# First stage of a diffusion layer kernel: squares in tiles of their own, eight tiles summed by TensorE instead of four, and a new order of its 528 steps

## The chip, the cores and the metric

The kernel runs on one core of a Trainium2 chip. What is measured is the device time of one execution in microseconds (us), as the median over several runs. A core has five engines, each with an instruction queue of its own that is worked in order: TensorE (PE in the profile; its weight loads are listed apart as PEld), VectorE (DVE), ScalarE (ACT), GpSimd (POOL) and SyncE (SP). In this kernel SP issues the loads, and 16 DMA engines carry them out.

## The reference

One layer of a diffusion transformer: 512 latent tokens and 256 context tokens of width 2048. Both are normalised and modulated, projected, attended in two ways, and go through a gated MLP. The change lies in the first lines alone:

```python
def _rmsnorm(x, w):
    xf = x.astype(jnp.float32)
    y = xf * lax.rsqrt(jnp.mean(xf * xf, axis=-1, keepdims=True) + EPS)
    return y.astype(x.dtype) * w
...
mod_x = (sc_ @ w_ada[l] + b_ada[l])[:, None, :]
mod_c = (scc @ w_ada[l] + b_ada[l])[None, None, :]
...
h = _modulate(_rmsnorm(x, norm1_w[l]), sh1, s1)
hc = _modulate(_rmsnorm(xc, norm1_w[l]), sh1c, s1c)
...
p = h @ w_in
```

So each token needs the sum of its 2048 squares, and each of the 2048 features needs a scale and a shift, which are dot products of the conditioning vectors with rows of `w_ada`.

## The kernel before, in words

The tokens stand in the free direction, the features in the 128 partitions: 16 feature tiles `kt`, each 512 latent columns (x) and 256 context columns (c) wide. Two neighbouring tiles make a pair; pair p holds tiles 2p and 2p+1. The first stage does the following.

- **Loads** (SP, lines 423 to 539): x in 16 loads of 256 KB into `a4k` tiles, the context in 8 loads into `c4k` tiles, then for each feature tile one row block of `w_ada` of 1 MB (`ada`, three buffers), for each pair four blocks `adak` of 512 KB (four buffers), and for each feature tile a weight block `wr` of 320 KB (two buffers).
- **Sum of squares.** For each pair ScalarE squares x (line 454) and, for pairs 0 to 3, the context (line 460); VectorE squares the context of pairs 4 to 7 (line 458). Pair 0 goes to the tile `ccb`, the others to two buffers `h` in turn. VectorE adds pairs 1 to 6 to `ccb`, one instruction of 1536 columns for each (line 465). TensorE then multiplies `ccb` and the last pair by a matrix of ones and adds up over partitions in a PSUM tile `s` (line 472: two column halves of 512 and 256 for each of two tiles of two pairs, 8 matmuls in all).
- **Wide rows.** TensorE spreads the two conditioning vectors over all partitions (line 487), and ScalarE copies them into the tiles `cb` and `ccb` (line 491). For the context vector the target is `ccb`, so this copy comes after TensorE has read the sum of squares there.
- **Root** (lines 502 to 511): ScalarE computes the reciprocal root by Ln and Exp (502, 504) and two factors (505, 507); VectorE sharpens it by one Newton step into `rinv` (509, 511), the 512 latent columns first, then the 256 context columns.
- **Scales and shifts.** Scale: TensorE multiplies the `adak` blocks (554), ScalarE copies (558), TensorE picks the columns (562), ScalarE finishes them (568). Shift of 14 of the 16 tiles: VectorE takes two dot products of 2048 columns with an `ada` block (619; one with `cb`, one with `ccb`). Shift of tiles 1 and 8 ("turned"): TensorE transposes the `ada` block in four groups (582), ScalarE copies each (585), TensorE multiplies (591), ScalarE copies (594), TensorE picks (599), ScalarE finishes (604).
- **Normalised tiles.** VectorE multiplies by `rinv` (640), ScalarE modulates (646) and rounds to the high part (652), VectorE takes the low part (654). The weights are split likewise (541 on ScalarE, 542 on VectorE).
- **Features.** For each of the 16 feature tiles TensorE does five groups of three matmuls with 512 latent columns and four groups of three with 256 context columns (`mm3`, lines 286 to 288). They add up in PSUM over the whole stage.

Every step is recorded in a list with a number, and `FIRST_ORDER` (line 74) is a table of these numbers: the steps are issued in its order, which fixes the order on every engine. After the first stage the kernel goes on with code that is the same in both versions.

Of the kernel before, what the change touches and what calls it, by code (L numbers as in the profile page):

```python
# [9 lines left out]
F32 = mybir.dt.float32  # L10
# [54 lines left out]
class Step:  # L65
# [6 lines left out]


FIRST_ORDER = (
# [24 lines left out]


ATTENTION_ORDER = (
# [83 lines left out]
class Flow:  # L185
# [7 lines left out]
    def buf(self, make, ring=None, count=None):  # L193
        if ring:
            self.rings[ring] = count
        return Buf(ring, make)
# [26 lines left out]
def layer_kernel(ctx: ExitStack, tc: tile.TileContext, small, rope, c_row, cc_row, x_t, ctx_t, ada, ada_k,  # L223
# [170 lines left out]
    def none():  # L394
        return buf(lambda: None)
# [14 lines left out]
    def xv(kts):  # L410
        return sel_(xr[kts[0] // 2], kts)

    def cv(kts):
        k = kts[0] % 2
        return cr[kts[0] // 4]()[:, kts[0] // 2 % 2, k:k + len(kts)]
# [17 lines left out]
    step("ACT", 1.3, 3.0, lambda: sc.preload_act_table_set("natural_log_exp_and_others"))  # L433
    step("ACT", 0.2, 3.1, lambda: sc.activation(ls, ls, AF.Exp))
    ssq = buf(s_tile, "s", 2)
    LAST = (7,)
    ON_DVE = (4, 5, 6, 7)

    def h_buf():
        return buf(lambda: st.tile([P, 2 * TT], F32, tag="h", name=nm("h"), bufs=2), "h", 2)  # L440

    def hv(t, kts, i):
        n_ = len(kts)
        if i:
            return t[:, 2 * T:2 * T + n_ * C].rearrange("p (k c) -> p k c", k=n_)
        return t[:, :n_ * T].rearrange("p (k t) -> p k t", k=n_)

    taken = buf(lambda: ccb)
    qs = [taken] + [h_buf() for _ in range(7)]
    for p in range(8):  # L450
        t, q, kts = 3.5 + 2 * p, qs[p], (2 * p, 2 * p + 1)
        flow.part = f"q{p}"
        for k in range(2):
            step("ACT", 0.63, t + 0.7 * k, lambda q=q, kts=kts, k=k: sc.square(hv(q(), kts, 0)[:, k], xv(kts)[:, k]),
                 r=[at_x[kts[k]]], w=[q], hold=[xr[p]])
        def ctx_square(q=q, kts=kts, p=p):
            if p in ON_DVE:
                ve.tensor_tensor(hv(q(), kts, 1), cv(kts), cv(kts), op=ALU.mult)
            else:
                sc.square(hv(q(), kts, 1), cv(kts))  # L460

        step(*(("DVE", 0.7) if p in ON_DVE else ("ACT", 0.64)), t + 0.6, ctx_square, r=[at_c[kts[0]], at_c[kts[1]]],
             w=[q], hold=[cr[p // 2]])
        if p and p not in LAST:
            step("DVE", 1.77, t + 1.8, lambda q=q: ve.tensor_tensor(
                ccb[:, :2 * TT], ccb[:, :2 * TT], q(), op=ALU.add), r=[q], w=[taken])
    flow.part = "q"
    sums = [0, *LAST]
    for i, p in enumerate(sums):
        for k in range(2):  # L470
            for m, (c0, c1, cost) in enumerate(((0, T, 1.0), (T, TT, 0.5))):
                step("PE", cost, 20.0 + i + 0.1 * k, lambda m=m, p=p, c0=c0, c1=c1, i=i, k=k: pe.matmul(
                    ssq()[:, c0:c1], ones32, hv(qs[p](), (0, 1), m)[:, k], start=i == 0 and k == 0,
                    stop=i == len(sums) - 1 and k == 1), r=[qs[p]], w=[ssq])
    wide = [[none() for _ in range(4)] for _ in range(2)]
    for i, t in enumerate((cb, ccb)):
        flow.part = f"b{i}"
        s_ = buf(s_tile, "s", 2)
        for j in range(4):
            d = s_ if j < 2 else buf(b_tile, "b", 4)  # L480

            def view(d=d, j=j):
                return d()[:, j * 512:j * 512 + 512] if j < 2 else d()

            def rows_of(i=i, j=j, view=view):
                for k in range(4):
                    pe.matmul(view()[:, k * P:(k + 1) * P], cpad[:, 4 * j + k, i:i + 1].to_broadcast([P, P]), ident,
                              start=True, stop=True)

            step("PE", 1.0, 5.0 + 18 * i + j, rows_of, r=[pad], w=[d])  # L490
            step("ACT", 0.57, 8.0 + 18 * i + j, lambda t=t, o=slice(j * 512, j * 512 + 512), view=view: sc.copy(
                t[:, o], view()), r=[d], w=[wide[i][j]] + [taken] * i)

    flow.part = "r"
    rinv = st.tile([P, TT], F32, name="rinv")
# [2 lines left out]
    for k, (c0, c1) in enumerate(((0, T), (T, TT))):  # L498
        r, s, g = rinv[:, c0:c1], slice(c0, c1), 1 - 0.38 * k
        br = none()  # L500
        t = 24.0 + 0.1 * k
        step("ACT", 0.7 * g, t, lambda r=r, s=s: sc.activation(r, ssq()[:, s], AF.Ln, bias=epst, scale=1.0 / D),
             r=[ssq], w=[br])
        step("ACT", 0.63 * g, t, lambda r=r: sc.activation(r, r, AF.Exp, scale=-0.5), w=[br])
        step("ACT", 0.65 * g, t, lambda s=s: sc.activation(nt[0]()[:, s], ssq()[:, s], AF.Identity, bias=epst, scale=1.0 / D),
             r=[ssq], w=[nt[0]])
        step("ACT", 0.65 * g, t, lambda r=r, s=s: sc.activation(nt[1]()[:, s], r, AF.Square, scale=math.sqrt(0.5)),
             r=[br, ssq], w=[nt[1]])
        step("DVE", 0.69 * g, t, lambda s=s: ve.tensor_tensor(nt[1]()[:, s], nt[1]()[:, s], nt[0]()[:, s], op=ALU.mult),
             r=[nt[0]], w=[nt[1]])  # L510
        step("DVE", 0.69 * g, t, lambda r=r, s=s: ve.scalar_tensor_tensor(
            out=r, in0=nt[1]()[:, s], scalar=1.5, in1=r, op0=ALU.subtract, op1=ALU.mult), r=[nt[1]], w=[br])
        at_r.append(br)
# [188 lines left out]
    step("X", 0.0, T0 + 200, lambda: None, needs=[s for s in flow.steps if s.eng == "PE"], hold=[*xh, *xl, *ch])  # L702
    with tc.manual_schedule(engines={mybir.EngineType.PE, mybir.EngineType.Activation, mybir.EngineType.DVE,
                                     mybir.EngineType.SP, mybir.EngineType.Pool}):
        for i in FIRST_ORDER:
            flow.steps[i].fn()
    ve.tensor_tensor(neglam, ls[:, 1:2], ls[:, 0:1], op=ALU.subtract)
# [1554 lines left out]
```

## Time and profile before

| | us |
|---|---|
| median of 3 runs (2326.39 to 2332.14) | 2327.16 |
| the profiled execution | 2327.31 |
| its span, from first to last instruction | 2325.5 |
| TensorE busy | 2288.4 (98%) |
| VectorE busy | 1725.2 (74%) |
| ScalarE busy | 1164.3 (50%) |

A row of a timeline gives the start in us from the span's start, the duration, the engine, the line, the operation and its operands (output<-inputs), then how many neighbouring instructions are merged, and in brackets the idle time ahead of it with what ended that. A row of the windows gives, for a stretch of time, its length, then the busy time of PE, PEld, DVE, ACT and POOL with the number of instructions, the share of full speed that the clock of TensorE was granted, the share of time in which the DMA engines were busy, and GB/s.

### The profile page before, as it was taken

To read this page: it belongs to the slowest core of one execution; us is meant where nothing else is said; L and a number is where in the kernel's file an instruction comes from. 1 tells how busy PE (TensorE), PEld (TensorE's weight loads), DVE (VectorE), ACT (ScalarE), POOL (GpSimd) and SP (SyncE) were. 2 spreads that over 40 slices of the span, in tenths; PEclk is the share of its full clock that TensorE was granted. 3 is DMA by queue.
4 is the path that set the end of the run, shared out by engine and by line. 5 is a ranking of instruction groups with operands and counts; after the bars stand their busy time and mean duration, and the time that the engine had idled before them with its cause. 6 is when DMAs were issued, how large, how long until landed. Compare 5 with 4: busy or idle time off the path is not lost.

```text
span 2325.5 us, 32178 instructions
## 1 busy us (share of the span) xinstructions
PE 2288.4 (98%) x12378; PEld 1959.2 (84%) x12378; DVE 1725.2 (74%) x2206; ACT 1164.3 (50%) x1777; POOL 265.6 (11%) x308
## 2 busy tenths in 40 slices
PE   6999999999999999999999999999999999999998
PEld 5788888888888888898888888888888888888887
DVE  7988775699877677796676758585858585867667
ACT  6542211577776522454554545454545454545455
POOL 0000001200133121000101010101010101010110
PEclk8999999999999999999999999999999999999999
DMA  9978888646201299335646463746464646554663
GB/s 360 366 259 303 317 296 292 183 132 210 81 25 37 96 348 359 104 117 136 148 126 143 130 161 101 175 114 160 121 154 127 142 131 145 141 144 123 159 184 102
DMA packets 124731, 404.23 MB, mean 174 GB/s; under 512 B 14337, under 2 KB 18945, under 8 KB 114081
## 3 DMA queue, kind: packets, MB, share of 16 engines
q1 hardware_dynamic: 96658, 346.92, 44.9%
q0 software_dynamic: 26768, 54.21, 12.6%
q8 instruction: 97, 1.59, 0.3%
q10 hardware_dynamic: 1152, 1.05, 0.1%
q14 instruction: 56, 0.46, 0.1%
HBM read 332.45 MB, written 69.67 MB: 173 GB/s over the span
## 4 chain that ended last, share of the span: by engine, by line
PE 94%; DVE 3%; ACT 1%; DMA 1%; issue 1%; SPq 0%; DVEq 0%; ACTq 0%
PE y L1959 12%; PE b L286 11%; PE b L287 11%; PE b L288 11%; PE y L1961 6%; PE z L1959 6%; PE s L1025 4%; PE s L286 3%; PE s L287 3%; PE s L288 3%; PE z L1961 3%; PE x L1959 3%; PE pt L1045 2%; PE f L286 2%; PE f L287 2%; PE f L288 2%
## 5 line engine op out<-in xcount | busy, mean ns | idle before, releaser
L1719 DVE TENSOR_TENSOR wl<-wr,wh 128x1024 fp32r<-128x1024 f32 x144 | 177.0, 1230 | 137.1 <-ACT wh L1711 136.4
L1984 POOL DMA_DIRECT2D x_d<-xs x160 | 139.6, 994 | 1148.4 <-ACT xs L1983 1146.4
L286 PE MATMUL b<-ah,wh 128*128 128x512 f32 (+1 forms) x664 | 256.8, 387 | 0.0
L287 PE MATMUL b<-al,wh 128*128 128x512 f32 (+1 forms) x664 | 256.7, 387 | 0.0
L1711 ACT CAST wh<-wr 128x1024 fp32r<-128x1024 f32 x144 | 150.7, 1048 | 211.3 <-PE b L287 100.9
L288 PE MATMUL b<-ah,wl 128*128 128x512 f32 (+1 forms) x664 | 255.8, 385 | 0.0
L1719 DVE TENSOR_TENSOR wl<-rb,wh 128x1024 fp32r<-128x1024 f32 x123 | 150.0, 1219 | 120.6 <-ACT wh L1711 120.6
L1719 DVE TENSOR_TENSOR wl<-ws,wh 128x1024 fp32r<-128x1024 f32 x123 | 150.4, 1222 | 110.6 <-ACT wh L1711 110.6
L1711 ACT CAST wh<-rb 128x1024 fp32r<-128x1024 f32 x123 | 129.2, 1051 | 174.1 <-PE b L287 80.0
L1959 PE MATMUL y<-a2k,wh 128*128 128x512 f32 x656 | 164.1, 392 | 0.4 <-DVE m L1658 0.4
L1711 ACT CAST wh<-ws 128x1024 fp32r<-128x1024 f32 x123 | 128.4, 1044 | 71.1 <-PE b L287 48.5
L288 PEld LDWEIGHTS b<-ah,wl 128*128 128x128 f32 x664 | 124.8, 188 | 25.7
L286 PEld LDWEIGHTS b<-ah,wh 128*128 128x128 f32 x664 | 125.1, 188 | 22.9
L287 PEld LDWEIGHTS b<-al,wh 128*128 128x128 f32 x664 | 125.1, 188 | 22.0
L1959 PEld LDWEIGHTS y<-a2k,wh 128*128 128x128 f32 x656 | 118.6, 189 | 22.2 <-issue 0.5
L250 ACT CAST wh<-wr 128x1024 fp32r<-128x1024 f32 x51 | 53.5, 1052 | 162.3 <-DMA wr<-in_w_o 47.8
L1959 PE MATMUL y<-b2k,wh 128*128 128x512 f32 x410 | 106.8, 390 | 0.0
L1983 ACT ACTIVATE xs<-b,modx 128x512 f32<-128x512 f32 x160 | 101.7, 681 | 5.4 <-DMA x_d<-xs 5.4
L1030 ACT ACTIVATE p<-s,m 128x768 f32<-128x768 f32 x96 | 86.6, 903 | 30.7 <-DVE m L1028 28.6
L1028 DVE TENSOR_REDUCE m<-s 128x1 f32<-128x768 f32 x96 | 90.6, 950 | 6.8 <-PE s L1025 6.4
L1961 PEld LDWEIGHTS y<-a2k,wl 128*128 128x128 f32 x656 | 89.5, 190 | 6.4
L1961 PE MATMUL y<-a2k,wl 128*128 128x256 f32 x656 | 91.5, 282 | 0.0
(530 smaller groups left out, 5929.9 us busy)
## 6 DMA issues: line engine op xcount, KB each, us to landing
ada<-in_ada SPq DMA_DIRECT2D x80, 1024.0 KB, 7.3
rb<-in_w_up SPq DMA_DIRECT2D x123, 512.0 KB, 4.4
wr<-in_w_dn SPq DMA_DIRECT2D x88, 512.0 KB, 3.6
x_d<-xs POOLq DMA_DIRECT2D x160, 256.0 KB, 6.0
wr<-in_w_up SPq DMA_DIRECT2D x53, 512.0 KB, 4.3
wr<-in_w_f SPq DMA_DIRECT2D x34, 512.0 KB, 6.3
adak<-in_ada_k SPq DMA_DIRECT2D x32, 512.0 KB, 7.8
wr<-in_w_o SPq DMA_DIRECT2D x32, 512.0 KB, 5.3
```

What stands on the lines that cost most here:

```text
L286: pe.matmul(out, st[0], mv[0], start=start, stop=False, **kw)
L287: pe.matmul(out, st[0], mv[1], start=False, stop=False, **kw)
L288: pe.matmul(out, st[1], mv[0], start=False, stop=stop, **kw)
L1025: pe.matmul(s()[:, c0:c1], a, b[:, c0:c1], start=i == 0, stop=i == len(ms) - 1)
L1028: step("DVE", 0.87, t + cost + 0.2, lambda: ve.tensor_reduce(out=m(), in_=s()[:, :TT], axis=AX.X, op=ALU.max, negate=True), r=[s], w=[m])
L1030: step("ACT", 0.9, t + cost + 1.2, lambda: sc.activation(p(), s()[:, :TT], AF.Exp, bias=m(), accum_out=lcol()), r=[s, m], w=[p, l], lag=0.25)
L1711: sc.copy(t, raw[:, k * n_:k * n_ + n_])
L1719: ve.tensor_tensor(t, raw[:, k * n_:k * n_ + n_], hi[k].bitcast(F32), op=ALU.subtract)
L1959: pe.matmul(o, w[j][0], hs[j], start=start and j == 0, stop=False, skip_group_check=True)
L1961: pe.matmul(o[:, h0], w[j][1], hs[j][:, h0], start=False, stop=j == 7, skip_group_check=True)
L1983: sc.mul(x, po, modx[:, 80 + dt:81 + dt])
L1984: gp.dma_start(x1_d[dt], x, accum_op=ALU.add)
```

## The change

The squares no longer go to `ccb` and `h`. Eight tiles `sx` (from the `a4k` buffers) and four tiles `sq_c` (from the `c4k` buffers) hold all of them, made ahead of everything else. VectorE does four additions of pairs instead of six: pair 0 to 1, 1 to 2, 2 to 3 and 4 to 5, each in two instructions (1024 columns of x, 512 of the context). TensorE multiplies four pairs by ones instead of two: 3, 5, 6 and 7, so 16 matmuls instead of 8. The x and context halves are waited for apart. The copies into `ccb` no longer wait for anything of the squares. Line numbers of the changed kernel are one to twelve higher: 423 is now 424, 472 is 482, 582 is 592, 619 is 629, 286 is 287.

```diff
-    LAST = (7,)
     ON_DVE = (4, 5, 6, 7)
+    ADDS = ((0, 1), (1, 2), (2, 3), (4, 5))
...
-    taken = buf(lambda: ccb)
-    qs = [taken] + [h_buf() for _ in range(7)]
+    sx, sq_c = [a4k(F32) for _ in range(8)], [c4k(F32) for _ in range(4)]
...
-        if p and p not in LAST:
-            step("DVE", 1.77, t + 1.8, lambda q=q: ve.tensor_tensor(
-                ccb[:, :2 * TT], ccb[:, :2 * TT], q(), op=ALU.add), r=[q], w=[taken])
...
+    for a, b in ADDS:
+        for i, cost in enumerate((1.22, 0.69)):
+            flow.part = f"q{b}"
+            step("DVE", cost, 5.3 + 2 * b, lambda a=a, b=b, i=i: ve.tensor_tensor(
+                square_of(b, i), square_of(b, i), square_of(a, i), op=ALU.add), r=[squares[i][a]], w=[squares[i][b]],
+                 hold=[homes[i][a], homes[i][b]])
+    sums = [none() for _ in range(2)]
+    roots = [p for p in range(8) if p not in [a for a, _ in ADDS]]
+    for p in roots:
         for k in range(2):
...
+                    ssq()[:, c0:c1], ones32, square_of(p, i)[:, k], start=p == roots[0] and k == 0,
+                    stop=p == roots[-1] and k == 1), r=[squares[i][p]], w=[sums[i]], hold=[ssq, homes[i][p]])
...
-                t[:, o], view()), r=[d], w=[wide[i][j]] + [taken] * i)
+                t[:, o], view()), r=[d], w=[wide[i][j]])
...
+        for b in (*sx, *sq_c):
+            b()
         for i in FIRST_ORDER:
             flow.steps[i].fn()
```

The table itself is new from end to end; its first line was

```diff
-    2, 0, 3, 6, 5, 1, 24, 4, 8, 11, 27, 65, 9, 30, 73, 7, 31, 10, 28, 29, 12, 71, 32, 14, 69, 34, 13, 33, 35, 20,
+    0, 22, 4, 6, 2, 24, 3, 5, 26, 89, 7, 50, 9, 27, 13, 32, 16, 83, 28, 8, 30, 75, 11, 31, 10, 51, 87, 1, 35,
```

On SP, these rows stood at the end of the x loads before (`wr`, `ada` and `adak` are the weight blocks of above):

```order
L425 DMA c4k_250<-in_ctx_t 128x512 x2
L423 DMA a4k_257<-in_x_t 128x512 x2
L539 DMA wr_268<-in_w_g 128x640
L539 DMA wr_273<-in_w_g 128x640
L527 DMA ada_276<-in_ada 128x2048
L527 DMA ada_285<-in_ada 128x2048
L532 DMA adak_295<-in_ada_k 128x1024
```

Now they are:

```order
L426 DMA c4k_188<-in_ctx_t 128x512
L549 DMA wr_237<-in_w_g 128x640
L424 DMA a4k_244<-in_x_t 128x512
...
L537 DMA ada_269<-in_ada 128x2048
L424 DMA a4k_282<-in_x_t 128x512
L424 DMA a4k_286<-in_x_t 128x512
...
L537 DMA ada_301<-in_ada 128x2048
L549 DMA wr_314<-in_w_g 128x640
L542 DMA adak_318<-in_ada_k 128x1024
L542 DMA adak_323<-in_ada_k 128x1024
L549 DMA wr_330<-in_w_g 128x640
```

One weight block and one `ada` block have moved ahead of the last four x loads. After `wr_330` come two more `adak` blocks and then `ada_343`, the block of the turned tile 1.

On VectorE, the end of the squares and the Newton step of the root before (`junk` marks a dot product, `modx` its result for latent, `modc` for context tokens; each is followed by a short instruction that is left out here):

```order
L465 TENSOR_TENSOR ccb<-ccb,h_279 128x1536
L542 TENSOR_TENSOR wl_300<-wr_268,wh_289 128x640
L542 TENSOR_TENSOR wl_307<-wr_273,wh_291 128x640
L458 TENSOR_TENSOR h_293<-c4k_250 128x512
...
L619 ISA junk_313,modx<-ada_276,cb,smt 128x2048
...
L619 ISA junk_326,modx<-ada_285,cb,smt 128x2048
...
L619 ISA junk_345,modc<-ada_276,ccb,smt 128x2048
...
L619 ISA junk_365,modc<-ada_285,ccb,smt 128x2048
...
L509 TENSOR_TENSOR h_362<-h_362,h_355 128x512
L511 SCALAR_TENSOR_TENSOR rinv<-h_362,rinv 128x512
```

and now:

```order
L464 TENSOR_TENSOR c4k_183<-c4k_186 128x512
L473 TENSOR_TENSOR a4k_177<-a4k_177,a4k_176 128x1024
L629 ISA junk_311,modx<-ada_269,cb,smt 128x2048
...
L629 ISA junk_325,modc<-ada_269,ccb,smt 128x2048
...
L629 ISA junk_335,modc<-ada_301,ccb,smt 128x2048
...
L629 ISA junk_345,modx<-ada_301,cb,smt 128x2048
...
L552 TENSOR_TENSOR wl_357<-wr_314,wh_341 128x640
L519 TENSOR_TENSOR h_359<-h_359,h_348 128x512
L521 SCALAR_TENSOR_TENSOR rinv<-h_359,rinv 128x512
L552 TENSOR_TENSOR wl_385<-wr_330,wh_362 128x640
L519 TENSOR_TENSOR h_359<-h_359,h_348 128x256
```

The Newton step still stands behind four dot products, but the second of them now takes the context vector, and one weight split stands ahead of the Newton step.

On TensorE, from the last sum of squares to the first features before (`b_335<-ident,ada` are the transposes of the turned tile, `c4k` and `a4k` the normalised tiles):

```order
L472 MATMUL s_297<-h_293,ones_85 128x256
L554 MATMUL b_335<-adak_295,cpad 32x256 x4
L554 MATMUL b_335<-adak_310,cpad 32x256 x4
L554 MATMUL b_335<-adak_304,cpad 32x256 x4
L554 MATMUL b_335<-adak_317,cpad 32x256 x4
L562 MATMUL b_335<-sel,row 128x2 x2
L582 MATMUL b_335<-ident,ada_330 128x128 x8
L591 MATMUL b_335<-wt_382,cpad 32x128 x8
L582 MATMUL b_335<-ident,ada_330 128x128 x4
L286 MATMUL s_432<-a4k_414,wh_289 128x512
```

and now:

```order
L482 MATMUL s_288<-a4k_179,ones_85 128x512 x2
L482 MATMUL s_288<-c4k_182,ones_85 128x256
L482 MATMUL s_288<-c4k_183,ones_85 128x256 x4
L564 MATMUL b_364<-adak_323,cpad 32x256 x4
...
L572 MATMUL b_364<-sel,row 128x2 x2
L592 MATMUL b_364<-ident,ada_343 128x128 x8
L287 MATMUL b_423<-c4k_410,wh_362 128x256
L288 MATMUL b_423<-c4k_410,wh_362 128x256
L289 MATMUL b_423<-c4k_410,wl_385 128x256
...
L601 MATMUL b_364<-wt_412,cpad 32x128 x8
```

Features of the context now stand between the groups of the turned tile, ahead of those of the latent tokens. From the first transpose of the turned tile 1 to the first products with `adak` blocks of the third pair, TensorE has the same instructions in both versions, in another order. In the rest of the stage the products with `adak` blocks stand further back among the features: those of the fourth pair at row 146 of TensorE's order instead of row 128, those of the fifth at 193 instead of 172, those of the seventh at 327 instead of 303.

More of the change, by code (lines that the diff above doesn't have):

```diff
@@ L446, in hv, with square_of @@
         return t[:, :n_ * T].rearrange("p (k t) -> p k t", k=n_)
-    taken = buf(lambda: ccb)
-    qs = [taken] + [h_buf() for _ in range(7)]
+    def square_of(p, i):
+        return sq_c[p // 2]()[:, p % 2] if i else sx[p]()
+    sx, sq_c = [a4k(F32) for _ in range(8)], [c4k(F32) for _ in range(4)]
+    squares = [[none() for _ in range(8)] for _ in range(2)]
+    homes = [sx, [sq_c[p // 2] for p in range(8)]]
     for p in range(8):
-        t, q, kts = 3.5 + 2 * p, qs[p], (2 * p, 2 * p + 1)
+        t, kts = 3.5 + 2 * p, (2 * p, 2 * p + 1)
@@ L452, in layer_kernel, with ctx_square @@
         flow.part = f"q{p}"
         for k in range(2):
-            step("ACT", 0.63, t + 0.7 * k, lambda q=q, kts=kts, k=k: sc.square(hv(q(), kts, 0)[:, k], xv(kts)[:, k]),
-                 r=[at_x[kts[k]]], w=[q], hold=[xr[p]])
-        def ctx_square(q=q, kts=kts, p=p):
+            step("ACT", 0.59, t + 0.7 * k, lambda p=p, kts=kts, k=k: sc.square(square_of(p, 0)[:, k], xv(kts)[:, k]),
+                 r=[at_x[kts[k]]], w=[squares[0][p]], hold=[xr[p], sx[p]])
+        def ctx_square(kts=kts, p=p):
@@ L457, in ctx_square @@
             if p in ON_DVE:
-                ve.tensor_tensor(hv(q(), kts, 1), cv(kts), cv(kts), op=ALU.mult)
+                ve.tensor_tensor(square_of(p, 1), cv(kts), cv(kts), op=ALU.mult)
             else:
-                sc.square(hv(q(), kts, 1), cv(kts))
-        step(*(("DVE", 0.7) if p in ON_DVE else ("ACT", 0.64)), t + 0.6, ctx_square, r=[at_c[kts[0]], at_c[kts[1]]],
-             w=[q], hold=[cr[p // 2]])
-        if p and p not in LAST:
-            step("DVE", 1.77, t + 1.8, lambda q=q: ve.tensor_tensor(
-                ccb[:, :2 * TT], ccb[:, :2 * TT], q(), op=ALU.add), r=[q], w=[taken])
@@ L467, in layer_kernel @@
-    flow.part = "q"
-    sums = [0, *LAST]
-    for i, p in enumerate(sums):
+                sc.square(square_of(p, 1), cv(kts))
+        step(*(("DVE", 0.7) if p in ON_DVE else ("ACT", 0.6)), t + 0.6, ctx_square, r=[at_c[kts[0]], at_c[kts[1]]],
+             w=[squares[1][p]], hold=[cr[p // 2], sq_c[p // 2]])
+    for a, b in ADDS:
[4 more added lines that the diff above has]
+                 hold=[homes[i][a], homes[i][b]])
@@ L470, in layer_kernel @@
+    sums = [none() for _ in range(2)]
+    roots = [p for p in range(8) if p not in [a for a, _ in ADDS]]
+    for p in roots:
+        flow.part = f"p{p}"
         for k in range(2):
[L471 to L474, printed above, removed]
+            for i, (c0, c1, cost) in enumerate(((0, T, 1.2), (T, TT, 0.62))):
+                step("PE", cost, 6.0 + 2 * p + 0.1 * k, lambda i=i, p=p, c0=c0, c1=c1, k=k: pe.matmul(
+                    ssq()[:, c0:c1], ones32, square_of(p, i)[:, k], start=p == roots[0] and k == 0,
+                    stop=p == roots[-1] and k == 1), r=[squares[i][p]], w=[sums[i]], hold=[ssq, homes[i][p]])
@@ L502, in layer_kernel @@
         step("ACT", 0.7 * g, t, lambda r=r, s=s: sc.activation(r, ssq()[:, s], AF.Ln, bias=epst, scale=1.0 / D),
-             r=[ssq], w=[br])
+             r=[sums[k]], w=[br], hold=[ssq])
         step("ACT", 0.63 * g, t, lambda r=r: sc.activation(r, r, AF.Exp, scale=-0.5), w=[br])
         step("ACT", 0.65 * g, t, lambda s=s: sc.activation(nt[0]()[:, s], ssq()[:, s], AF.Identity, bias=epst, scale=1.0 / D),
-             r=[ssq], w=[nt[0]])
+             r=[sums[k]], w=[nt[0]], hold=[ssq])
         step("ACT", 0.65 * g, t, lambda r=r, s=s: sc.activation(nt[1]()[:, s], r, AF.Square, scale=math.sqrt(0.5)),
-             r=[br, ssq], w=[nt[1]])
+             r=[br], w=[nt[1]])
         step("DVE", 0.69 * g, t, lambda s=s: ve.tensor_tensor(nt[1]()[:, s], nt[1]()[:, s], nt[0]()[:, s], op=ALU.mult),
```

47 rows, old and new, of the table FIRST_ORDER are left out of this document.

## The prediction

> **What bounds the kernel now.** I read the page first, then the busy time by stretches, then the timelines of the first 60 us. The page:
>
> ```profile
> span 2325.5 us, 32178 instructions
> ...
> PE 2288.4 (98%) x12378; PEld 1959.2 (84%) x12378; DVE 1725.2 (74%) x2206; ACT 1164.3 (50%) x1777; POOL 265.6 (11%) x308
> ```
>
> TensorE idles 2325.5 - 2288.4 = 37.1 us in all. The stretches say where (the fourth column is PE's busy time, then PEld, DVE, ACT, POOL, the granted clock, the DMA share and GB/s):
>
> ```profile
> 10.00:20.00 10.00, 5.14 (x37) 4.76 (x35) 8.96 (x7) 8.47 (x17) 0.00 (x0) 0.92 1.05 405
> 20.00:30.00 10.00, 6.35 (x14) 3.55 (x15) 9.82 (x11) 4.59 (x8) 0.00 (x0) 0.57 1.02 424
> 30.00:40.00 10.00, 7.01 (x73) 4.39 (x71) 8.05 (x11) 7.99 (x17) 0.00 (x0) 0.95 1.01 391
> 40.00:50.00 10.00, 8.28 (x59) 6.53 (x52) 9.23 (x13) 4.78 (x11) 0.00 (x0) 0.71 1.00 380
> 53.00:147.00 94.00, 93.45 (x679) 74.95 (x678) 86.99 (x89) 51.05 (x88) 1.46 (x2) 1.00 0.86 318
> 147.00:300.00 153.00, 153.00 (x718) 127.83 (x717) 124.60 (x172) 45.02 (x67) 0.00 (x0) 1.00 0.81 293
> ```
>
> From 53 us on TensorE is full. What the change can win lies ahead of that: idle time of TensorE, and work done at a clock of 0.57 or 0.71. After the stage, TensorE has the same instructions in the same order in both kernels and no idle time in the 153 us that follow, so I let whatever the first stage gains pass through to the end unchanged. The early path on TensorE (start, duration, idle time ahead in brackets):
>
> ```profile
> 23.65 5.31 PE L472 MATMUL s<-ccb,ones 128*128 128x512 f32 x8 [6.54 <-DVE ccb L465]
> ...
> 30.54 1.89 PE L472 MATMUL s<-h,ones 128*128 128x256 f32 x6
> 32.36 1.93 PE L554 MATMUL b<-adak,cpad 128*32 128x256 f32 x32
> 35.23 0.61 PE L562 MATMUL b<-sel,row 128*128 128x2 f32 x4 [0.93 <-ACT row L558]
> 36.54 0.66 PE L582 MATMUL b<-ident,ada 128*128 128x128 f32 x4 [0.70 <-ACT a L568]
> 37.87 0.66 PE L582 MATMUL b<-ident,ada 128*128 128x128 f32 x4 [0.68 <-ACT wt L585]
> 39.20 1.08 PE L591 MATMUL b<-wt,cpad 128*32 128x128 f32 x16 [0.68 <-ACT wt L585]
> 42.00 1.11 PE L582 MATMUL b<-ident,ada 128*128 128x128 f32 x4 [1.72 <-ACT row L594]
> ...
> 58.44 1.07 PE L554 MATMUL b<-adak,cpad 128*32 128x256 f32 x16
> ...
> 146.85 0.40 PE L286 MATMUL b<-a4k,wh 128*128 128x512 f32 x1
> ```
>
> It waits 6.54 us for the additions of the squares, then step by step for the chain of the turned tile between TensorE and ScalarE. The row at 58.44 is the first product of the third pair, that at 146.85 the first instruction behind the stage. From 36.54 to 58.44 both kernels have the same TensorE instructions, and from 58.44 to 146.85 again, so I compare the two at 58.44.
>
> **The change part by part.** *VectorE* (rows of its timeline):
>
> ```profile
> 21.74 1.76 DVE L465 TENSOR_TENSOR ccb<-ccb,h 128x1536 f32<-128x1536 f32 x1
> 23.42 1.55 DVE L542 TENSOR_TENSOR wl<-wr,wh 128x640 fp32r<-128x640 f32 x2
> 24.89 0.69 DVE L458 TENSOR_TENSOR h<-c4k 128x512 f32<-128x512 f32 x1
> ...
> 25.75 2.34 DVE L619 CUSTOM_DVE_ANT_0 junk<-ada,cb,smt 128x2048 bf16<-128x2048 f32 x1
> ...
> 28.13 2.35 DVE L619 CUSTOM_DVE_ANT_0 junk<-ada,cb,smt 128x2048 bf16<-128x2048 f32 x1
> ...
> 32.34 2.35 DVE L619 CUSTOM_DVE_ANT_0 junk<-ada,ccb,smt 128x2048 bf16<-128x2048 f32 x1 [1.85 <-ACT ccb L491]
> ...
> 37.01 0.69 DVE L509 TENSOR_TENSOR h<-h,h 128x512 f32<-128x512 f32 x1
> 37.73 0.69 DVE L511 SCALAR_TENSOR_TENSOR rinv<-h,rinv 128x512 f32<-128x512 f32 x1
> ...
> 42.42 1.22 DVE L640 TENSOR_TENSOR h<-a4k,rinv 128x1024 f32<-128x1024 f32 x1
> ```
>
> Six additions of 1.76 become four of 1.22 + 0.69, taking for them the rows of the same widths (1024 in L640, 512 in L458): 10.6 us become 7.6. The four squares stay. These 3.0 us are not the gain as such. What counts is when the four dot products are through, since the Newton step of the root (37.01) stands behind them. Before, the first started at 25.75, and the third waited 1.85 us because `ccb` still held the sum of squares. That wait goes. What is late next is the load of the `ada` blocks:
>
> ```profile
> 14.41 0.94 SPq L423 DMA_DIRECT2D a4k<-in_x_t  x2
> ...
> a4k<-in_x_t SPq DMA_DIRECT2D x16, 256.0 KB, 5.2
> ```
>
> The last x tile was issued at about 15 us and landed some 5.2 later, at 20.2. By the 405 to 424 GB/s of the windows a 256 KB tile takes 0.64 us, a weight block 0.8, an `adak` block 1.25, an `ada` block 2.5. In the new order the first `ada` block lands after 20 instead of 24 tiles and one weight block: 20.2 - 4 x 0.64 + 0.8 + 2.5 = 20.9. Then come four x tiles (the last at 23.5, 3.3 us later than before) and the second `ada` block (26.0). Dot products follow each other at 28.13 - 25.75 = 2.38: two from 20.9 to 25.7, two from 26.0 to 30.8, then a split of weights (half of the 1.55, 0.8) to 31.6. The Newton step starts at 31.6 instead of 37.0.
>
> *TensorE's sum of squares* doubles. The row at 30.54 (two of 256 columns and one of 512, 1.89) gives 0.9 and 0.45 at full clock, so 8 x 0.9 + 8 x 0.45 = 10.8 us instead of 5.4. The first eight of these wait for VectorE's additions and fit in the time in which the loads still arrive. Behind the last x tile lie four of 512 and five of 256: from 23.5 to 27.1 for x and 29.4 for the context. ScalarE then needs four operations ahead of Newton:
>
> ```profile
> 20.25 1.28 ACT L433 ACT_TABLE_LOAD   x1
> ...
> 32.47 0.69 ACT L502 ACTIVATE rinv<-s,epst 128x512 f32<-128x512 f32 x1 [0.16 <-PE s L472]
> ...
> 34.28 0.63 ACT L507 ACTIVATE h<-rinv 128x512 f32<-128x512 f32 x1
> 34.82 0.35 ACT L558 COPY row<-b 128x256 f32<-128x256 f32 x1
> ...
> 37.23 0.59 ACT L585 COPY wt<-b 128x512 f32<-128x512 f32 x1
> ```
>
> That is 34.28 + 0.63 - 32.47 = 2.4 us. Ahead of them on ScalarE stands the split of a weight block that lands at 26.8, so they run from 27.5 to 29.9, and Newton's 31.6 stands: the doubled sum costs nothing. The cover is 1.7 us. At half clock x would be through at 30.7, ScalarE at 33.1, and 1.5 us would be lost. A third table load (1.28, as in the row at 20.25) falls in the wait for the first x tile.
>
> *Start of the turned tile.* Its `ada` block lands 3712 KB after the second one, at 26.0 + 9.3 = 35.3, and its scale is no sooner: the last `adak` block lands at 32.7, half of the products stand behind it (1.0, half of the 1.93), then the copy (0.35 and hand-over, 0.4; the 0.93 of before held a queue on ScalarE), the pick (0.61) and the finish (0.70), which is 35.4. So the transposes start at 35.4 instead of 36.54: 1.2 us gained, less than the 5.4 on VectorE, because now a load is last.
>
> *From there to the third pair's products.* Before: 58.44 - 36.54 = 21.9 us, with waits of 0.68, 0.68 and 1.72. In the new order two transposes are parted by a copy (0.59 and hand-over, 0.95 in all); the next products find context features of tile 0 in front of them, and these need `rinv` for the context and the normalised tile. Newton at 31.6 plus five operations of VectorE and ScalarE puts them at 36.2, ahead of TensorE's 37.5. One more wait of about 0.4 stays. That is 1.4 instead of 3.1: 1.7 gained. If ScalarE hands over as slowly as before, nothing is gained here; if every gap is filled, 3.1.
>
> *The clock* lies over this stretch:
>
> ```profile
> 36.00:38.00 2.00, 0.79 (x5) 0.55 (x6) 1.97 (x4) 1.87 (x6) 0.00 (x0) 1.00 0.97 344
> 38.00:40.00 2.00, 1.32 (x20) 0.88 (x20) 1.97 (x4) 1.09 (x3) 0.00 (x0) 0.73 1.00 369
> 40.00:42.00 2.00, 0.28 (x8) 0.00 (x1) 1.77 (x5) 1.65 (x4) 0.00 (x0) 0.50 0.92 246
> 42.00:44.00 2.00, 2.00 (x7) 1.81 (x8) 2.00 (x4) 1.44 (x3) 0.00 (x0) 0.50 0.99 388
> 44.00:46.00 2.00, 2.00 (x9) 1.51 (x8) 2.00 (x1) 0.00 (x0) 0.00 (x0) 0.56 1.05 423
> ```
>
> TensorE was at half clock from about 39 to 45.8 and worked some 4.8 us of it, so 2.4 were lost. In the new order it is slack between 29.4 and 35.4 (it waits there for `adak` blocks and the scale), so I expect the clock to fall at 32 to 36, and, with work nearly without gaps from 35.4, to rise again near 42, having cost 2.0: 0.4 gained. If it never falls, 2.4 are gained; if it stays low until 45.8 as before, some 9 us of work are slow and 4.5 lost, 2.1 worse than before.
>
> [...]
>
> *Later in the stage* the products with `adak` blocks stand further back:
>
> ```profile
> PEld b L554 <- DMA adak<-in_ada_k: 1.6, 3, 0.7
> ```
>
> Before, between 53 and 147 us they waited 1.6 us in all for their loads. In the new order three of them stand 18 to 24 rows further back, and the buffers of the loads ahead of theirs come free as VectorE gets through its dot products, 4.9 us sooner. So I let this wait go: 1.6, between 0 and 1.6.
>
> The sum: 1.2 + 1.7 + 0.4 + 1.6 = 4.9 us. The profiled execution took 2327.31, its span 2325.5 plus 1.8 around it; 4.9 off gives 2322.4. The median of the three runs, 2327.16, is the same to 0.15, so I predict 2322.3.
>
> **The rivals.**
> 1. *The clock falls only after a long idle stretch* (as between 17 and 23.65, where 6.54 us of idling went with 0.57), and not after short gaps. Then 2.0 more: 2320.3, with all gaps filled as well 2318.9. Against it stands the drop at 39. [...]
> 2. *The clock stays low to 45.8.* Start earlier, but slow: 2.5 off the gain, 2324.8. For it: the clock at 40 to 44 did not rise before some 3.5 us of full work.
> 3. *VectorE becomes the bound, slower than before.* From 20.9 on it has 28 dot products (66.6 us by 2.38), 15 weight splits (some 11.5), and about 30 of normalising and low parts: to 129, plus 3 for the last `ada` block, whose buffer comes free late. TensorE has 2.9 us behind the last of it. With VectorE's idle time of before (94.00 - 86.99 = 7.0 between 53 and 147), the stage ends at 142, which still fits my sum (146.9 - 4.9). Each us of idling beyond that is lost. It decides against the change from 12 us on; with twice the 7.0, 14, it is 2 to 3 us slower: 2330. For it: by these sums VectorE has hardly 1 us to spare. Against: it starts its dot products 4.9 us earlier.
> 4. *It does not do what it says*: the stage's end hangs on its last loads, which are bound by free buffers, and the earlier start dries up there: 2327. The DMA share of 0.86 between 53 and 147 speaks against it.
>
> **How the numbers follow.** Forecast 0.60, rival 1 0.16, rival 2 0.12, rival 3 0.06, rival 4 0.06. A change under 0.3% (7.0 us), about what a measurement of this kernel tells from none, counts as the same. Faster by more needs rival 1 with its gaps filled, or the upper end of my bounds (1.2 + 3.1 + 2.4 + 1.6 = 8.3 us): 0.10 from rival 1 and 0.08 from the forecast, 0.18. Slower by more needs rival 3 with over 19 us of idling: 0.03. The rest, 0.79, is the same. My bounds downward: 1.2 + 0 - 2.1 + 0 - 1.5 = -2.4, so 2329.6; that all ends fall together is unlikely, and I close the range at 2328.0. Upward, 8.3 gives 2319.0, and I go to 2318.5.
>
> **What would show it.** In the new trace: the first dot product near 20.9 and Newton's first step near 31.6; the sum of squares at full clock and done by 29.4; the transposes of the turned tile from 35.4; the first product of the third pair near 55.1 at about 3.3 us ahead of 58.44; a clock that is low between about 34 and 42; no wait of the `adak` products for loads; the stage's last features 4.9 us earlier than 146.9. I am wrong if the Newton step is not 4 us earlier, if VectorE idles over 10 us between 53 and 147, or if the rest of the kernel does not keep the lead.

## The result and the profile after

The changed kernel took 2349.3 us (median of 4 runs, 2347.02 to 2350.09), the kernel before 2329.02 beside it (4 runs, 2326.39 to 2332.14): a ratio of 1.009, 95% interval 1.0078 to 1.0103. I had forecast 2322.3, with a range of 2318.5 to 2328.0. The kernel became 20 us slower; the prediction was wrong in its sign and outside its range. (The new table has 538 entries; the 528 of the title is the length of the old one.)

The page of after, to be set beside that of before:

```profile
span 2346.6 us, 32211 instructions
...
PE 2296.6 (98%) x12394; PEld 1964.8 (84%) x12394; DVE 1721.0 (73%) x2208; ACT 1164.7 (50%) x1778; POOL 265.5 (11%) x308
```

The span grew by 21.1 us and TensorE's busy time by 8.2 (it has eight matmuls more, and some of its work takes longer: the first score below 0.76 us instead of 0.47), so TensorE now idles 50.0 us instead of 37.1. Shares of the span show neither. The stretches do (columns as before: length, busy time of PE, PEld, DVE, ACT, POOL, granted clock, DMA share, GB/s):

```profile
38.00:40.00 2.00, 2.00 (x18) 1.76 (x20) 2.00 (x2) 1.51 (x3) 0.00 (x0) 0.57 0.98 408
40.00:42.00 2.00, 2.00 (x24) 1.60 (x16) 2.00 (x4) 0.27 (x1) 0.00 (x0) 0.58 1.03 420
...
53.00:147.00 94.00, 93.82 (x680) 75.68 (x679) 83.72 (x90) 51.62 (x92) 1.46 (x2) 1.00 0.85 322
147.00:300.00 153.00, 153.00 (x717) 127.88 (x717) 125.06 (x170) 43.29 (x63) 0.00 (x0) 1.00 0.82 298
...
400.00:410.00 10.00, 10.00 (x45) 8.28 (x45) 1.23 (x1) 1.05 (x1) 0.00 (x0) 1.00 0.01 2
...
420.00:430.00 10.00, 0.00 (x0) 0.00 (x0) 1.68 (x3) 0.73 (x2) 5.69 (x8) 0.53 1.02 344
430.00:440.00 10.00, 6.57 (x22) 5.45 (x23) 2.54 (x3) 1.05 (x1) 0.00 (x0) 0.62 1.04 281
```

Before, two of these stretches read:

```profile
400.00:410.00 10.00, 10.00 (x46) 8.29 (x45) 1.23 (x1) 1.05 (x1) 0.00 (x0) 1.00 1.06 236
...
420.00:430.00 10.00, 9.92 (x46) 7.97 (x46) 6.70 (x9) 4.53 (x7) 8.94 (x12) 1.00 1.03 399
```

Up to 300 us there is no loss: the first stage has gained, 3.5 of the 4.9 us forecast. The loss begins where I had not looked: TensorE does nothing at all between 420 and 430. And the row that explains it comes earlier: from 400 to 410 TensorE is full, yet the DMA engines move almost nothing (share 0.01, before 1.06). The loads have stopped.

First what the first stage did, on TensorE:

```profile
21.13 5.46 PE L482 MATMUL s<-a4k,ones 128*128 128x512 f32 x12 [0.85 <-DVE a4k L473]
...
28.36 0.70 PE L482 MATMUL s<-c4k,ones 128*128 128x256 f32 x2 [1.34 <-ACT h L515]
29.84 1.56 PE L482 MATMUL s<-c4k,ones 128*128 128x256 f32 x6 [0.78 <-ACT rinv L512]
...
36.34 0.66 PE L592 MATMUL b<-ident,ada 128*128 128x128 f32 x4 [0.69 <-ACT a L578]
37.75 0.66 PE L592 MATMUL b<-ident,ada 128*128 128x128 f32 x4 [0.75 <-ACT wt L595]
...
42.90 0.66 PE L592 MATMUL b<-ident,ada 128*128 128x128 f32 x4 [0.38 <-ACT wt L595]
...
55.59 1.07 PE L564 MATMUL b<-adak,cpad 128*32 128x256 f32 x16
...
143.39 0.40 PE L287 MATMUL b<-a4k,wh 128*128 128x512 f32 x1
```

and on VectorE, the first dot product and Newton's first step:

```profile
21.24 2.35 DVE L629 CUSTOM_DVE_ANT_0 junk<-ada,cb,smt 128x2048 bf16<-128x2048 f32 x1 [0.17 <-DMA ada<-in_ada]
...
31.73 0.68 DVE L519 TENSOR_TENSOR h<-h,h 128x512 f32<-128x512 f32 x1
```

The first product of the third pair came 2.85 us earlier than before (58.44), the first instruction behind the stage 3.46 us earlier (146.85). Then, at the start of the attention, TensorE of after:

```profile
418.18 0.39 PE L289 MATMUL b<-wh,a4k 128*128 128x512 f32 x1
433.43 0.76 PE L1037 MATMUL s<-ks,qs 128*128 128x512 f32 x1 [14.86 <-DMA ks<-k_d]
...
448.53 0.79 PE L1037 MATMUL s<-ks,qs 128*128 128x512 f32 x1 [4.67 <-ACT p L1042]
```

and before at the same place, the last product, the first and the third score:

```profile
421.64 0.39 PE L288 MATMUL b<-wh,a4k 128*128 128x512 f32 x1
422.10 0.47 PE L1025 MATMUL s<-ks,qs 128*128 128x512 f32 x1
...
431.04 0.50 PE L1025 MATMUL s<-ks,qs 128*128 128x512 f32 x1 [0.49 <-ACT p L1030]
```

The last product ahead of the scores still comes 3.5 us earlier than before, and then the first score waits 14.86 us for its keys `ks`. The third waits 4.67 more for ScalarE. Who is late behind these? SyncE's queue, after and then before (`qs` are the two tiles of queries of the first head, in this order):

```profile
390.84 26.73 SPq L1111 DMA_DIRECT2D qs<-q_d  x2
...
419.45 0.62 SPq L1119 DMA_DIRECT2D ks<-k_d  x1
...
425.92 1.73 SPq L987 DMA_DIRECT2D wr<-in_w_f  x1
```

```profile
397.01 1.05 SPq L1099 DMA_DIRECT2D qs<-q_d  x2
...
399.93 0.62 SPq L1107 DMA_DIRECT2D ks<-k_d  x1
...
402.61 0.52 SPq L975 DMA_DIRECT2D wr<-in_w_f  x1
```

Two loads that took 1.05 us to issue now take 26.73. The waits of SyncE's queue say on whom:

```profile
SPq L1111 <- PE s L289: 25.8, 1, 25.8
```

The second query load waits for TensorE's last reading of a context tile: that reading ended at 417.21 and the load was out by 417.57 (390.84 + 26.73). The keys and the weight block stand behind it in the queue. The late weight block is also the second wait: ScalarE's queue has the split of two weight blocks ahead of the exponential `p` that the third score needs.

```profile
438.19 1.05 ACT L999 CAST wh<-wr 128x1024 fp32r<-128x1024 f32 x1 [17.46 <-DMA wr<-in_w_f]
446.54 1.04 ACT L999 CAST wh<-wr 128x1024 fp32r<-128x1024 f32 x1 [7.30 <-DMA wr<-in_w_f]
447.49 0.89 ACT L1042 ACTIVATE p<-s,m 128x768 f32<-128x768 f32 x1
```

Why should a query tile wait for a context tile? In the addresses of the two built programs, the second query tile lies over one of the eight 4 KB buffers that held `c4k` tiles, released shortly before. In the kernel before, that buffer last held the context features of pair 4, in the changed one those of pair 7. TensorE reads the pairs in turn, so pair 4 is through three pairs ahead of pair 7, the last. (Even before there was no margin: TensorE was through pair 4 at 397.55, just as the second load's turn came.) The change took four more `c4k` buffers for the squares ahead of everything; so the features of the eight pairs came to other buffers, and pair 7 under the query tile. No line of the attention changed.

The loss adds up. In the changed kernel TensorE waits 14.86 + 4.67 = 19.5 us here. Behind the two waits it works at half clock (0.50 between 434 and 437 and between 449 and 454; a product of 512 columns follows the one ahead of it by 0.43 us there, by 0.23 at full clock), for 4.2 us (433.4 to about 437.6) and for 6.2 us (448.5 to about 454.7), which loses half of that, 5.2 us. Together that is 24.7 us. The profiled span is 23.7 us longer than that of e1_slot_p0 below, the changed kernel with another placement.

### The profile page after: what moved, and what is told of

Read it like the earlier page. It is cut to its first block, busy times and chain, and to the rows that moved or that the text cites. A ratio compares the mean times of both kernels' runs of the same rounds, so it can differ in the third digit from the quotient of the medians.

```text
span 2346.6 us, 32211 instructions
## 1 busy us (share of the span) xinstructions
PE 2296.6 (98%) x12394; PEld 1964.8 (84%) x12394; DVE 1721.0 (73%) x2208; ACT 1164.7 (50%) x1778; POOL 265.5 (11%) x308
## 3 DMA queue, kind: packets, MB, share of 16 engines
q10 hardware_dynamic: 1152, 1.05, 0.1%
## 4 chain that ended last, share of the span: by engine, by line
PE 79%; issue 12%; DMA 3%; DVE 3%; POOL 2%; ACT 1%; SPq 0%; POOLq 0%; DVEq 0%; ACTq 0%
PE y L1971 9%; PE b L287 9%; PE b L288 9%; PE b L289 9%; PE y L1973 5%; PE z L1971 5%; PE s L1037 4%; PE s L287 3%; PE s L289 3%; PE s L288 3%; PE z L1973 2%; PE x L1971 2%; PE pt L1057 2%; PE f L287 2%; PE f L288 2%
## 5 line engine op out<-in xcount | busy, mean ns | idle before, releaser
L287 PEld LDWEIGHTS b<-ah,wh 128*128 128x128 f32 x664 | 125.2, 189 | 22.7
L1040 DVE TENSOR_REDUCE m<-s 128x1 f32<-128x768 f32 x96 | 90.8, 951 | 25.1 <-PE s L1037 24.7
```

What stands on the lines that cost most here:

```text
L287: pe.matmul(out, st[0], mv[0], start=start, stop=False, **kw)
L1040: step("DVE", 0.87, t + cost + 0.2, lambda: ve.tensor_reduce(out=m(), in_=s()[:, :TT], axis=AX.X, op=ALU.max, negate=True), r=[s], w=[m])
```

## The experiments

**Theory A**: placement. One load waits for the last reader of what lay at its address, and blocks SyncE's queue. **Rival B**: the new first stage itself, its order or traffic, causes the stall later on. In the built programs the `c4k` buffer touched first gets the lowest address, the one under the query tile. A fill of one column by GpSimd ahead of the stage therefore moves the buffers, and leaves everything else alone.

| kernel | pair under the query tile | query loads issued by | first score | third score | median |
|---|---|---|---|---|---|
| before | 4 | 398.06 | 422.10 | 431.04 | 2327.43 |
| changed | 7 | 417.57 | 433.43 | 448.53 | 2349.3 |
| e1_slot_p0: changed, moved | 0 | 393.02 | 418.80 | 427.79 | 2324.99 |
| e2_before_p7: before, moved | 7 | 420.35 | 434.61 | 450.72 | 2349.68 |
| e4_slot_p6: changed, moved | 6 | 412.86 | 423.27 | 441.39 | 2340.15 |
| e3_qs_late: changed, load behind | 7 | 419.08 | 420.15 | 430.99 | 2329.05 |

(Runs of the kernel before beside the changed kernel took 2329.02, beside the others 2327.43. The times of loads and scores are those of one profiled execution each.)

**e1_slot_p0.**

```diff
+        for b in (sq_c[0], cr[3], cr[2]):
+            nc.gpsimd.memset(b()[:, 0, 0, 0:1], 0.0)
         for i in FIRST_ORDER:
             flow.steps[i].fn()
```

> The changed kernel, with three one-column fills by GpSimd ahead of everything else, which touch three of the context tiles first and so set which buffer lies where. Nothing else differs: now the buffer under the second query tile holds the context features of pair 0 instead of pair 7, the buffers of pairs 6 and 7 lie highest. Theory A (placement: SyncE's queue stands at the load of the second query tile until TensorE has read the last context features, and all loads behind it come late): the load issues with the first one near 391, the first score starts near 418.6, no waits of 14.9 and 4.7 us there, and the time is the before's less the 3.5 us of the first stage: 2325.5, against 2329.0 and 2349.3. Rival B (the new first stage itself, its order and its traffic, brings the later stall about): the wait stays in some form and the time stays near 2349. Rival C (both have a part): between 2330 and 2345.

Measured: 2324.99 (11 runs) against 2327.43; ratio 0.9994, interval 0.9985 to 1.0003. SyncE's queue and TensorE:

```profile
391.98 1.04 SPq L1113 DMA_DIRECT2D qs<-q_d  x2
```

```profile
418.80 0.47 PE L1039 MATMUL s<-ks,qs 128*128 128x512 f32 x1
...
427.79 0.50 PE L1039 MATMUL s<-ks,qs 128*128 128x512 f32 x1 [0.49 <-ACT p L1044]
```

The wait is gone, the first score stands where A put it, and the whole loss is back: 24.3 us between the medians, 22.7 when each is taken from its own runs of the kernel before. B falls, and with it C, in which both have a part: the whole new first stage is in this kernel.

**e2_before_p7.** The converse, on the kernel before.

```diff
+        nc.gpsimd.memset(cr[3]()[:, 0, 0, 0:1], 0.0)
         for i in FIRST_ORDER:
             flow.steps[i].fn()
```

> The kernel before, its first stage unchanged, with one one-column fill by GpSimd ahead of everything, which touches the last context tile first, so that the buffer under the second query tile holds the context features of pair 7 instead of pair 4. Theory A: the load waits for TensorE's last reading of pair 7, near 420.9 instead of 397.6; the first score starts some 15.8 us behind that (as 417.66 and 433.43 stood in the changed kernel), near 436.7 instead of 422.1, with the rest of the loss of the changed kernel behind it: about 23.8 us slower than before, 2352.8. Rival B: as before, 2329.0. Rival C: between 2335 and 2348.

Measured: 2349.68 against 2327.43, ratio 1.0097, interval 1.0084 to 1.0111. SyncE's wait and the scores:

```profile
SPq L1100 <- PE s L288: 24.8, 1, 24.8
```

```profile
434.61 0.77 PE L1026 MATMUL s<-ks,qs 128*128 128x512 f32 x1 [13.25 <-DMA klz<-k_d]
...
450.72 0.79 PE L1026 MATMUL s<-ks,qs 128*128 128x512 f32 x1 [5.87 <-ACT p L1031]
```

One column filled by an idle engine costs the kernel before 22 us: the same two waits, without any part of the change. A gave 2352.8; it was 3 too high, the first score came 14.3 us after the load and not 15.8.

**e3_qs_late.** In the attention's table, step 5 (the second query load) moves behind 6 (keys), 141 (weight block) and 48 (next keys); both query tiles are still made at step 4, so that the addresses stay.

```diff
-    0, 4, 5, 2, 1, 3, 6, 7, 8, 49, 50, 10, 11, 141, 142, 48, 47, 51, 52, 143, 53, 54, 55, 144, 145, 146, 9, 12,
+    0, 4, 2, 1, 3, 6, 7, 8, 49, 50, 141, 48, 5, 10, 11, 142, 47, 51, 52, 143, 53, 54, 55, 144, 145, 146, 9, 12,
```

> The changed kernel with its placement kept (the second query tile still over pair 7's buffer, the same wait of its load), but this load is issued behind the first keys, one weight block and the second keys instead of ahead of them. It tells the blocked queue from the late tile itself. Theory A: the keys and the weight block are in time, the load still issues near 417.2 and lands some 3.5 us later, near 420.7; only the second score has to wait for it, about 2 us, and the values and weights behind it come 5 us later than they could: 2327 to 2331. Rival D (what costs the time is that this one query tile is late, whatever stands behind it): near 2349. Rival B: near 2349 as well.

Measured: 2329.05 against 2327.43, ratio 1.0006, interval 0.9998 to 1.0015. SyncE's queue, then TensorE:

```profile
396.18 0.62 SPq L1120 DMA_DIRECT2D ks<-k_d  x1
...
418.74 0.34 SPq L1111 DMA_DIRECT2D qs<-q_d  x1
```

```profile
420.15 0.47 PE L1037 MATMUL s<-ks,qs 128*128 128x512 f32 x1
...
422.29 0.39 PE L1037 MATMUL s<-ks,qs 128*128 128x512 f32 x1
...
430.99 0.50 PE L1037 MATMUL s<-ks,qs 128*128 128x512 f32 x1 [2.38 <-ACT p L1042]
```

The load still waits for pair 7 and is issued at 418.74. It costs 4 us against e1_slot_p0 instead of 24. Of the 4.0 us between the two profiled spans, 1.35 are there ahead of the first score (420.15 against 418.80), which waited for nothing, and 1.9 are the third score's longer wait for ScalarE (2.38 against 0.49). So it is not the late tile that costs the time, but what stands behind it in an in-order queue. Rival D falls as well. The next keys, which lie over the buffer of pair 6, waited in the same way (12.3 us, out at 411.94), and TensorE never waited for them.

**e4_slot_p6.** As e1_slot_p0, with the single fill on `cr[2]`.

> The changed kernel with one one-column fill, so that the buffer under the second query tile holds pair 6's context features instead of pair 7's. TensorE has read pair 6 about 8.2 us ahead of pair 7, so the load issues near 409.4 instead of 417.7. Theory A, as a matter of dose: the first score starts near 409.4 + 15.8 = 425.2 instead of 433.4, and of the 23.8 us lost by the changed kernel against a good placement 8 to 17 come back: 2332 to 2341, in between the two. Rival B: near 2349. A theory by which only pair 7 matters: 2325.5.

Measured: 2340.15, ratio 1.0061, interval 1.0047 to 1.0074. SyncE's queue, TensorE and ScalarE:

```profile
392.18 20.68 SPq L1112 DMA_DIRECT2D qs<-q_d  x2
```

```profile
423.27 0.47 PE L1038 MATMUL s<-ks,qs 128*128 128x512 f32 x1 [2.61 <-DMA klz<-k_d]
...
441.39 0.79 PE L1038 MATMUL s<-ks,qs 128*128 128x512 f32 x1 [8.07 <-ACT p L1043]
```

```profile
439.40 1.04 ACT L1000 CAST wh<-wr 128x1024 fp32r<-128x1024 f32 x1 [11.96 <-DMA wr<-in_w_f]
```

Less delay, less loss: 15.2 us instead of 24. The load came at 412.9 and not at 409.4: TensorE was through pair 6 at 412.50, 6.8 us ahead of pair 7 (419.30) and not 8.2, and all of that 2.1 us later than in the trace of the changed kernel (417.21). Most of the loss is now the weight blocks (8.07 us through ScalarE), not the keys (2.61).

With the placement put right, three kernels ask where the first stage's gain comes from, and a fourth is e1_slot_p0 again. They were measured together, against 2328.37 of the kernel before (33 runs). The mark of each is the start of the third pair's first product.

**e5_two_roots.** On e1_slot_p0, with the new steps put in at their places in the table:

```diff
-    ADDS = ((0, 1), (1, 2), (2, 3), (4, 5))
+    ADDS = ((0, 1), (1, 2), (2, 3), (4, 5), (3, 5), (5, 6))
```

> On top of the good placement of e1_slot_p0: the new tiles and the new order, but VectorE does two more additions of pairs (3 to 5, 5 to 6), so that TensorE multiplies two pairs by ones as before the change, 8 matmuls instead of 16. Theory: the doubled sum costs TensorE nothing, the additions cost VectorE what they take (2 x (1.22 + 0.69) = 3.8 us, of which it idled 0.6 ahead of the first dot product). So Newton's first step comes some 3 us later than 31.7, the first product of the third pair at 57.5 to 59 instead of 55.4, and the time is 2 to 3.5 us above that of e1_slot_p0: 2327 to 2328.5. Rival: the 5.4 us of matmuls that it saves are on the path, then the third pair stands at 55.4 or sooner and the time at 2322 to 2325.

Measured: 2328.92 (11 runs), ratio 1.0006, interval 0.9997 to 1.0016. TensorE's sum of squares, VectorE's Newton step, and the third pair:

```profile
25.08 5.65 PE L481 MATMUL s<-a4k,ones 128*128 128x512 f32 x8 [10.26 <-DVE a4k L472]
...
57.40 1.07 PE L563 MATMUL b<-adak,cpad 128*32 128x256 f32 x16
```

```profile
34.28 0.69 DVE L518 TENSOR_TENSOR h<-h,h 128x512 f32<-128x512 f32 x1 [0.95 <-ACT h L516]
```

TensorE waits 10.26 us for the additions, and the third pair's products come at 57.40, 2.0 us later than in e1_slot_p0 (55.44) and 1.4 later than in the same kernel measured beside it (55.97, e8_slot_again). The eight extra matmuls of the change cost less than the two additions that they replace. The mark is 0.1 short of what I expected, the time 0.4 above. But its profiled execution lost 2.0 us more in a place that the change does not touch, and e1_slot_p0 only 0.1 there (the same stretch of e5_two_roots, then of e1_slot_p0):

```profile
900.00:930.00 30.00, 27.96 (x121) 22.20 (x120) 21.59 (x20) 7.48 (x10) 7.65 (x8) 1.00 0.92 352
```

```profile
900.00:930.00 30.00, 29.86 (x132) 24.41 (x131) 23.31 (x23) 8.66 (x11) 7.68 (x8) 1.00 0.92 337
```

The control below lost 2.4 us there too. So I go by the mark: 1.4 to 2.0 us for the two additions. Behind the mark more is lost: at 129.34 TensorE waits 1.76 us for VectorE's low part of a tile, so that the first instruction behind the stage comes at 146.72, against 142.86 and 144.44 in the two executions of e1_slot_p0's kernel. How much of the 3.7 to 3.9 us between the medians that is, one execution does not show.

**e6_old_order.** On e1_slot_p0: the table of before, renumbered, without the two additions that are gone and with the sums of pairs 3, 5 and 6 where those of `ccb` stood.

> On top of the good placement: the new tiles, four additions and four sums, but the steps of the first stage in the order of before (the two additions that are gone left out, the new sums put where the old ones stood). It parts the tiles from the new order. If the tiles and the freed copy into the wide context row carry the gain, VectorE saves 3.0 us of additions and the wait of 1.85 us, and the first product of the third pair moves from 58.4 to 55.5 or so, as with the new order: 2324 to 2325. If the order carries it, the mark stays at 58 to 58.5 and the time at 2327 to 2328. I expect something in between, 56 to 57.5, since the turned tile's chain between TensorE and ScalarE keeps its gaps in the old order: 2325.5 to 2327.

Measured: 2330.38 (11 runs), ratio 1.0013, interval 1.0003 to 1.0023. VectorE and the third pair:

```profile
31.90 2.35 DVE L628 CUSTOM_DVE_ANT_0 junk<-ada,ccb,smt 128x2048 bf16<-128x2048 f32 x1 [3.19 <-ACT ccb L500]
```

```profile
58.13 1.07 PE L563 MATMUL b<-adak,cpad 128*32 128x256 f32 x16
```

My expectation of something in between was wrong: the third pair moves by 0.3 us alone, less than the 0.5 by which the two executions of e1_slot_p0's kernel differ, and the time is no better than before. (Its profiled execution took 2327.97, in line with the mark; why the median lies 2 us above the kernel before is not shown.) The third dot product still waits for `ccb`, 3.19 us now, because TensorE makes these rows behind the sums in this order. Own tiles only permit the copy to go first; the order does it. So the gain at the third pair, 2.2 to 2.7 us against the two executions of e1_slot_p0's kernel, needs the order; whether the order alone would do without the tiles was not tried.

**e7_before_fills.** The control: the kernel before with fills on `cr[0]`, `cr[3]`, `cr[2]`, pair 4 still under the query tile.

> The kernel before with three one-column fills by GpSimd, which keep pair 4 under the second query tile and lay the buffers of the last pairs highest. Control for the fills and for the placement above the query tile: in the kernel before nothing waits there, so theory A says no change, 2326.5 to 2328.5 against 2327.4. If the better placement as such is worth the 2.4 us that e1_slot_p0 showed, it is 2325.

Measured: 2328.14 against 2328.37, ratio 1.0006, interval 0.9997 to 1.0015. No change, as A says: the fills, and the buffers of the last pairs laid highest, give the kernel before nothing where no load waits.

**e8_slot_again.** The kernel of e1_slot_p0 once more.

> The kernel of e1_slot_p0 once more, beside the three others and against fresh runs of the kernel before, for its interval: 2324 to 2326, 1.5 to 3.5 us under the kernel before, third pair at 55.4.

Measured: 2325.25 (11 runs) against 2328.37, ratio 0.9991, interval 0.9982 to 1.0000; the third pair at 55.97. Twice, then, 2.4 and 3.1 us below the kernel before by the medians, and the intervals end at 1.0003 and 1.0000: it beats the changed kernel by some 23 to 24 us, and the kernel before by a little at most.

## Why the prediction was wrong

**The step that failed** is this: "After the stage, TensorE has the same instructions in the same order in both kernels and no idle time in the 153 us that follow, so I let whatever the first stage gains pass through to the end unchanged." The instructions were the same, and the 153 us were full in both. What differed was which buffer lay at which address, and with it what a load 390 us into the kernel waits for: it held SyncE's queue for 25.8 us, and the two waits of TensorE behind it (14.86 and 4.67 us), with the half clock behind each, took the lead and 20 us more. "The same instructions in the same order" says nothing on waits where tiles share memory. None of my rivals contained it; the closing remark "if the rest of the kernel does not keep the lead" named the place and no mechanism. With the placement put right, the time was 2324.99 and 2325.25, inside my range, with 2.4 and 3.1 us gained instead of 4.9. e1_slot_p0 and e2_before_p7 show the cause from both sides.

**The steps of the first stage**, forecast against the changed kernel's trace:

- First dot product 20.9: 21.24. Newton 31.6: 31.73. These held.
- Sum of squares done by 29.4: it ended at 31.4. The context half waited 1.34 and 0.78 us while ScalarE read the latent half of the same tile, which I had not counted. "The doubled sum costs nothing" still held: Newton was on time, and TensorE's next waits behind the sum (0.29 and 0.58 us) were for `adak` loads. e5_two_roots alone shows no more than that the sum costs less than two additions.
- Transposes at 35.4: 36.34, so 0.2 us earlier than before and not 1.2. The products behind the last `adak` load started at 33.48 as soon as it had landed; I had put that at 32.7.
- Clock: I expected 0.4 gained. The two windows from 38 to 42 with 0.57 and 0.58 make 2 x (0.43 + 0.42) / 0.5 = 3.4 us at half clock (0.50 between 39 and 41), all of it filled with work: 1.7 lost instead of 2.4, 0.7 gained.
- Waits from there to the third pair: 0.75 and 0.38 instead of 3.1, so 2.0 gained instead of 1.7.
- Third pair at 55.1: 55.59, 2.85 us gained of 3.3 (0.2 + 0.7 + 2.0).
- Waits of the `adak` products behind that: 1.6 forecast, 0.6 gained (3.46 - 2.85). The term was mis-sized in the forecast: these are waits of TensorE's weight loads (PEld), partly hidden behind its matmuls, which idled only 94.00 - 93.45 = 0.55 us in that stretch. The stage's lead was 3.5 us, not 4.9.
- VectorE: 94.00 - 83.72 = 10.3 us of idling, over the 10 that I had called a failure, and TensorE was full all the same (93.82 of 94.00). Rival 3 did not happen, and my threshold for it was no good test. But its premise, that VectorE has hardly 1 us to spare, shows: at 126 to 129 us TensorE waited for it, 0.18 us in this trace, 1.19 in e3_qs_late with the same stage, 1.76 in e5_two_roots with two additions more.
- How steady the lead is: the first instruction behind the stage came between 142.86 and 145.49 in the five profiled executions of the new stage, and between 146.1 and 146.9 in the three of the old one. The means are 2.2 us apart; 3.5 is one pair of executions.

**The clock.** It fell at about 38.3, and TensorE's gaps in the 3 us ahead were 0.69 and 0.75; in the kernel before it fell at about 39, and the longest gap in the 4 us ahead was 0.93. So in both traces it fell behind short gaps, against rival 1. In the 14.86 us of idling ahead of 433.43, TensorE's last product ended at 418.57, and a clock of 0.53 between 420 and 430 puts the fall at 420.6 (9.4 of the 10 us at half clock), 2.0 us later. In the next wait it fell at 447.9 (0.94 between 447 and 448), 4.0 us behind the last product. Full clock was back 4.2 us behind the first wait (0.62 between 430 and 440 puts it at 437.6) and 6.2 us behind the second (0.65 between 454 and 455 puts it at 454.7); in the first stage it took 3.4 us, from 38.3 to 41.7. What sets these times is not shown.

**What stays open**: why some executions lose 2 us between 900 and 930 (in e5_two_roots TensorE waits there 1.23 us for a weight block on ScalarE and 0.54 for one on VectorE; why these are late was not tried), why the end of the first stage scatters by 2.6 us, and the median of e6_old_order.

## What to carry to other kernels

Ask of a change not only which instructions it moves, but which buffers it takes: every later tile that shares that memory inherits another last reader, and the load into it another wait, here one of 25.8 us, 390 us into the kernel. Look for it in the waits of the DMA queues and in a DMA share that falls to nothing (here 0.01) while the compute engine is full. That sign alone proves no loss: in e1_slot_p0 the share is 0.01 between 430 and 440 as well, and TensorE is busy for 9.94 of the 10 us. An early load into memory that comes free late belongs behind the loads that need not wait (e3_qs_late: 2329.05 instead of 2349.3), or over a buffer that was read first (e1_slot_p0: 2324.99).

## What had not been expected of the hardware

The blocked queue showed late: the DMA share was 0.01 from 400 to 410 while TensorE was full, and TensorE stopped only at 418.6, 28 us after the queue reached the two query loads (390.84). And the price of TensorE's idling had a second part here: behind 14.86 us of waiting its matmuls ran at half clock for 4.2 us, and behind another 4.67 us of waiting for 6.2 us, together 5.2 us of work lost on top of the 19.5 us of waiting.
